# Seven products for eight in the first layer of a four-layer decoder trunk

## The chip, the cores and the metric

The kernel runs on one core of one Trainium2 chip. The metric is device time in microseconds (us) of one execution. The engines are named as the profile names them: PE is TensorE (matmuls, with PEld for the loads of its stationary operand), DVE is VectorE, ACT is ScalarE, POOL is GpSimd, and SP is SyncE, which here issues all the DMAs.

## The reference, cut to what matters

Four residual layers with different token mixers work on x of 1024 tokens by 1024 features. The change touches the first one, the gated convolution mixer:

```python
def conv_mixer(h, w_in, w_conv, w_out):
    proj = h @ w_in                                   # 1024 x 1024 by 1024 x 4096
    b_gate, c_gate, v, z = jnp.split(proj, 4, axis=-1)
    y = b_gate * causal_conv(c_gate * v, w_conv)      # 3 taps along the tokens
    return (y * jax.nn.silu(z)) @ w_out

def reference(x, ...):
    for i in range(DEPTH):
        h = rms_norm(x, norm_w[i])
        ...
        x = x + y.astype(x.dtype)
    return rms_norm(x, final_norm_w)
```

## The kernel before

Features lie on partitions and tokens on the free axis. There are 8 chunks of 128 features (`c`), and the tokens fall into two halves of 512 (`HT`). To keep fp32 precision each operand of a projection is split into a rounded high part and a low rest: ACT casts (`whi`, `hhi`), and POOL (for weights, `split_w`, L137) or DVE (for activations, L288) subtracts (`wlo`, `hlo`). A projection of one 128-column slice of weights on one half (`proj_steps`, L153 to L155) is then 8 chunks times 3 matmuls of 512 columns: high by high, high by low, low by high.

`start` loads x, transposes it on PE, normalises it (DVE L281, ACT L283, DVE L288) and leaves `hhi`, `hlo` for both halves; the first half's are ready first, and PE begins on it while DVE normalises the second.

`layer_conv` goes over 8 feature chunks `f` of the layer's width. For each it projects c, v, b and z on both halves, 8 projections in all. ACT copies c out of PSUM (`cs`, L451), DVE multiplies v by it (`u`, L456), ACT and DVE apply the three taps (L461 to L463), DVE multiplies by b (L468), ACT applies SiLU to z (L476) and DVE writes the gated result into `Y` (L477). The input x waits in DRAM (`xd`, `residual`) for the output projection. During `f == 2` `rope_tables` computes tables for layer 4 on DVE and ACT.

In the last chunk ACT and DVE split the finished `Y` into `hhi`, `hlo` again (`split_y`), and `out_half` projects them with `w_out`; its first three projections take the 7 chunks that are ready before the eighth.

Weights pass through pools of fixed depth: three raw tiles (`wraw`), six pairs `whi`, `wlo` (`WB = 6`), and PSUM has three `pj` tiles, two `sc`, one `ov` and two `tr`. Each engine runs its instructions strictly in the order written down for it. A scheduler writes that order when the program is built; in `start` and in the output projection the order on PE (in `start` that on ACT and DVE too) follows the code.

## Time and profile before

| | before |
|---|---|
| time, median of 3 runs | 2196.29 us (2195.63 to 2200.45) |
| profiled execution: time / span | 2195.09 / 2193.3 us |
| PE busy | 2110.1 us, 96% of the span, 11861 matmuls |
| DVE busy | 1235.0 us, 56% |
| ACT busy | 952.0 us, 43% |
| POOL busy | 784.7 us, 36% |

The span runs from the first to the last instruction; the profiled execution took 1.79 us more than its span. Matmuls overlap in the pipeline, so a matmul's own duration is longer than the distance from one start to the next, and it is that distance which adds up. DVE instructions overlap in the same way by a little: the distance between two starts is the cost of one in a row of them.

### The profile page before, as it was taken

How to read it: one execution, taken by the hardware profiler on the slowest of the kernel's cores; microseconds unless marked ns; L12 is line 12 of the kernel's file. 1: busy time of each engine (PE TensorE's matmuls, PEld its weight loads, DVE VectorE, ACT ScalarE, POOL GpSimd, SP SyncE). 2: the span in 40 equal slices, each digit the busy share in tenths (PEclk: the TensorE clock that was granted, in tenths of full speed). 3: DMA queues.
4: the chain of work that ended last, by engine and by line, in shares of the span. 5: the costliest groups of instructions: out<-in, count | busy, mean ns of one | idle time of the engine just before them, and what ended most of it. 6: DMA issues, size and time to landing. Idle time of an engine off the chain costs nothing.

```text
span 2193.3 us, 33426 instructions
## 1 busy us (share of the span) xinstructions
PE 2110.1 (96%) x11861; PEld 1776.1 (81%) x11861; DVE 1235.0 (56%) x2752; ACT 952.0 (43%) x2407; POOL 784.7 (36%) x685
## 2 busy tenths in 40 slices
PE   8999999999999999999999889999999998988998
PEld 6888888788898989888687677788887787777788
DVE  6141213452635445375454968775566658898874
ACT  6222113432433333354365443434444456666764
POOL 2222222651122121235355653322325544444630
PEclk9999999999999999999999999999999999999999
DMA  6121112551121321135356563333325421111124
GB/s 223 57 72 48 49 48 62 185 140 38 39 48 39 38 54 35 47 99 171 90 150 193 152 178 94 100 102 90 96 74 183 146 66 44 44 49 44 44 80 152
DMA packets 285772, 200.97 MB, mean 92 GB/s; under 512 B 41093, under 2 KB 245286, under 8 KB 285606
## 3 DMA queue, kind: packets, MB, share of 16 engines
q1 hardware_dynamic: 285606, 198.84, 31.9%
q8 instruction: 94, 1.54, 0.3%
q14 instruction: 72, 0.59, 0.1%
HBM read 152.51 MB, written 41.03 MB: 88 GB/s over the span
## 4 chain that ended last, share of the span: by engine, by line
PE 73%; DVE 13%; DMA 5%; ACT 3%; issue 3%; POOL 2%; SPq 1%; ACTq 0%; POOLq 0%; DVEq 0%
PE ps_pj L153 18%; PE ps_pj L154 18%; PE ps_pj L155 18%; PE ps_tr L647 1%; PE ps_pj L555 1%; PE ps_pj L557 1%; PE ps_pj L556 1%; DVE cu L1120 1%; DVE sp L1241 1%; DVE lg L963 1%; PE ps_tr L1135 1%; PE ps_ov L660 1%; PE ps_ov L659 1%; DMA acc<-ra 1%; DVE ra L776 1%
## 5 line engine op out<-in xcount | busy, mean ns | idle before, releaser
L153 PE MATMUL ps_pj<-hhi,whi 128*128 128x512 f32 (+2 forms) x2096 | 849.9, 406 | 1.8 <-ACT hhi L283 0.9
L154 PE MATMUL ps_pj<-hlo,whi 128*128 128x512 f32 (+2 forms) x2096 | 819.8, 391 | 3.6 <-DVE hlo L211 2.9
L155 PE MATMUL ps_pj<-hhi,wlo 128*128 128x512 f32 (+2 forms) x2096 | 819.4, 391 | 0.0
L137 POOL TENSOR_TENSOR wlo<-wraw,whi 128x512 fp32r<-128x512 f32 x308 | 419.5, 1367 | 782.5 <-ACT whi L136 773.7
L155 PEld LDWEIGHTS ps_pj<-hhi,wlo 128*128 128x128 f32 (+1 forms) x2096 | 394.8, 188 | 84.6
L154 PEld LDWEIGHTS ps_pj<-hlo,whi 128*128 128x128 f32 (+1 forms) x2096 | 396.2, 189 | 73.1 <-DVE hlo L211 4.6
L153 PEld LDWEIGHTS ps_pj<-hhi,whi 128*128 128x128 f32 (+1 forms) x2096 | 395.8, 189 | 72.3 <-issue 1.9
L136 ACT CAST whi<-wraw 128x512 fp32r<-128x512 f32 (+1 forms) x316 | 193.5, 617 | 379.5 <-PE ps_pj L154 288.2
L1120 DVE SCALAR_TENSOR_TENSOR cu<-cb,taps,cu 128x512 f32<-128x512 f32 x144 | 134.5, 934 | 12.2 <-ACT cu L1118 10.3
L972 POOL TENSOR_TENSOR lg<-lg,st 128x512 f32<-128x512 f32 (+1 forms) x64 | 64.1, 1002 | 119.8 <-DVE st L971 71.1
L700 ACT ACTIVATE lg<-lg,mx 128x512 f32<-128x512 f32 (+2 forms) x96 | 58.7, 613 | 64.6 <-DVE mx L695 64.3
L966 ACT ACTIVATE lg<-lg,st 128x256 f32<-128x256 f32 (+1 forms) x128 | 62.8, 491 | 49.8 <-DVE st L963 48.4
L652 ACT CAST phi<-ps_tr 128x512 fp32r<-128x512 f32 (+1 forms) x80 | 40.6, 544 | 94.8 <-PE ps_tr L647 94.8
L332 DVE TENSOR_TENSOR y<-ps_pj,xr 128x512 f32<-128x512 f32 x56 | 38.5, 688 | 73.1 <-PE ps_pj L155 61.5
L456 DVE TENSOR_TENSOR u<-ps_pj,cs 128x512 f32<-128x512 f32 x16 | 11.1, 691 | 114.9 <-PE ps_pj L155 112.3
L653 DVE TENSOR_TENSOR plo<-ps_tr,phi 128x512 fp32r<-128x512 f32 (+1 forms) x80 | 49.5, 633 | 42.5 <-ACT phi L652 42.5
L340 DVE TENSOR_TENSOR acc<-acc,hf 128x512 f32<-128x512 f32 x49 | 52.0, 1061 | 37.8 <-ACT hf L339 37.7
L986 PE MATMUL ps_ov<-phi,vv 128*128 128x256 f32 x120 | 32.7, 293 | 29.4 <-DVE o L993 27.8
L1241 DVE TENSOR_TENSOR sp<-sT,sU 128x504 f32<-128x504 f32 (+18 forms) x80 | 56.6, 707 | 6.4 <-DMA sU<-gLT 5.3
L963 DVE CUSTOM_DVE_ANT_0 lg<-ps_sc,band,sk 128x256 f32<-128x256 f32 (+1 forms) x128 | 54.9, 464 | 6.3 <-PE ps_sc L959 4.5
L477 DVE TENSOR_TENSOR y<-t,sz 128x512 f32<-128x512 f32 x16 | 15.9, 994 | 69.1 <-ACT sz L476 69.0
L555 PE MATMUL ps_pj<-whi,hhi 128*128 128x256 f32 x192 | 54.8, 285 | 0.0
(365 smaller groups left out, 3889.0 us busy)
## 6 DMA issues: line engine op xcount, KB each, us to landing
wraw<-in_conv_w_in_dram SPq DMA_DIRECT2D x64, 256.0 KB, 2.8
xd<-y SPq DMA_DIRECT2D x64, 256.0 KB, 3.4
wraw<-in_fox_w_in_dram SPq DMA_DIRECT2D x60, 256.0 KB, 4.2
xr<-xd SPq DMA_DIRECT2D x56, 256.0 KB, 3.0
wraw<-in_gdn_w_in_dram SPq DMA_DIRECT2D x52, 256.0 KB, 3.5
wraw<-in_swa_w_in_dram SPq DMA_DIRECT2D x40, 256.0 KB, 3.0
wraw<-in_conv_w_out_dram SPq DMA_DIRECT2D x32, 256.0 KB, 3.1
wraw<-in_fox_w_out_dram SPq DMA_DIRECT2D x32, 256.0 KB, 2.9
```

What stands on the lines that cost most here:

```text
L136: nc.scalar.copy(hi[:, :, :cols], raw[:, :, :cols])
L137: (eng or nc.gpsimd).tensor_tensor(lo[:, :, :cols], raw[:, :, :cols], hi[:, :, :cols].bitcast(F32), op=ALU.subtract)
L153: nc.tensor.matmul(o, hi, xhi, start=(c == 0), stop=False)
L154: nc.tensor.matmul(o, hi, xlo, start=False, stop=False)
L155: nc.tensor.matmul(o, lo, xhi, start=False, stop=(c == NC_ - 1))
L555: nc.tensor.matmul(ps, xhi, whi, start=(c == 0), stop=False)
L700: nc.scalar.activation(lg[:, :w], lg[:, :w], AF.Exp, bias=m, scale=-1.0, accum_out=su[:, t:t + 1])
L963: nc.vector.tensor_tensor_reduce(lg[:, u, :n], ps[:, u, :n], band[:, 2 * P - n:], 1.0, sk[:, 1, hd:hd + 1], ALU.add, ALU.min, st[:, 0, u:u ...
L966: nc.scalar.activation(lg[:, u, :n], lg[:, u, :n], AF.Exp, bias=st[:, 0, u:u + 1], scale=-1.0, accum_out=st[:, 1, u:u + 1])
L972: nc.gpsimd.tensor_tensor(lg[:, :, :n], lg[:, :, :n], st[:, 3, :].unsqueeze(2).broadcast_to([P, 2, n]), op=ALU.mult)
L1120: eng.scalar_tensor_tensor(u, cb[:, j:j + HT], tap(j), u, op0=ALU.mult, op1=ALU.add)
L1241: nc.vector.tensor_tensor(v, T[:, n0:i, n0:n1].rearrange("p j n -> p n j"), U[:, n0:i, i].unsqueeze(1).broadcast_to([P, n, m]), op=ALU.mult)
```

## The change

The first two feature chunks stay as they were. For the other six, the projections are taken two at a time (c with v, then b with z), and each pair is computed as a product of 2 by 2 blocks: the weight matrix falls into input halves (chunks 0 to 3, chunks 4 to 7) by two slices, and the activations into the same input halves by the two token halves. Strassen's method in Winograd's form does this with seven products of 12 matmuls where eight stood (`quad_steps`); a pair on both halves is called a quad here.

The sums that it needs are made elsewhere. Four mixtures of activations (`mixtures`, 16 pairs of a high and a low tile) are made once, on DVE with ACT's casts, from the normalised fp32 activations: those of the second half are kept (`self.last`), those of the first are computed again from `Y` and the kept row of scales (`self.rb`). They stand in the place of `Y` and of x's tiles. Four mixtures of weights per quad are made by DVE (`split_quad`), and each of the seven operands is split by ACT and POOL as weights were before. The products are summed in PSUM where they can be, and else by ACT copies and DVE additions (`p1`, `p5`, `u2`).

Since `Y` is taken, the gated results of the first two chunks and of all second halves go to DRAM (`yd`) and come back during the last quad; five first halves are kept in tiles of `hhi`, `hlo` that the quads no longer read. All eight chunks of x are written to `xd` at once, before the first chunk. `rope_tables` moves to `f == 3`.

```diff
+    def mixtures(self, p, layer):
+        nc = self.nc
+        self.mix = [[], [], [], []]
+        m0 = []
+        def first_half(c, t):
+            nc.vector.scalar_tensor_tensor(t, self.Y[c][0], self.col("norm_w", layer * NC_ + c), self.rb[0],
+                                           op0=ALU.mult, op1=ALU.mult)
+            return t
+        def keep(m, t, hi, lo):
+            nc.scalar.copy(hi, t)
+            nc.vector.tensor_tensor(lo, t, hi.bitcast(F32), op=ALU.subtract)
+            self.mix[m].append((hi, lo))
...
+        for i in range(4):
+            t = first_half(i, self.tmp("xr" if i % 2 else "hf", 2))
+            nc.vector.tensor_tensor(t, self.last[i], t, op=ALU.subtract)
+            m0.append(t)
+            keep(0, t, *(self.place("y", i, half, F32R) for half in range(NH)))
+            yield
+        for i in range(4):
+            h10 = first_half(i + 4, p.tile([P, HT], F32, name="e", bufs=EB))
+            nc.vector.tensor_tensor(m0[i], self.last[i + 4], m0[i], op=ALU.subtract)
+            keep(1, m0[i], *(self.place("y", i + 4, half, F32R) for half in range(NH)))
+            yield
+            nc.vector.tensor_tensor(h10, h10, m0[i], op=ALU.subtract)
+            keep(3, h10, *wide())
+            yield
+        m2 = []
+        for i in range(4):
+            m2.append(self.tmp("xr" if i % 2 else "hf", 2))
+            nc.vector.tensor_tensor(m2[i], self.last[i + 4], self.last[i], op=ALU.subtract)
+        yield
+        for i in range(4):
+            keep(2, m2[i], *wide())
+            yield
+    def raw_quad(self, p, src, a, b):
...
+        own = lambda: p.tile([P, 4, P], F32, name="wr", bufs=4)
+        shared = lambda: self.wp.tile([P, 4, P], F32, name="wraw", bufs=3)
+        return [load(own(), 0, a), load(shared(), 1, b), load(own(), 0, b), load(shared(), 1, a)]
+    def split_quad(self, p, raws):
+        a0, b1, b0, a1 = raws
+        yield self.split_w(a0, P)
+        s1 = p.tile([P, 4, P], F32, name="ws", bufs=2)
+        nc.vector.tensor_tensor(s1, b0, b1, op=ALU.add)
+        yield self.split_w(s1, P)
+        nc.vector.tensor_tensor(b0, a0, b0, op=ALU.subtract)
+        nc.vector.tensor_tensor(a0, s1, a0, op=ALU.subtract)
+        yield self.split_w(a0, P)
+        yield self.split_w(a1, P)
+        yield self.split_w(b0, P)
+        nc.vector.tensor_tensor(a1, a1, a0, op=ALU.subtract)
+        yield self.split_w(a1, P)
+        yield self.split_w(b1, P)
+    def quad_steps(self, p, ws):
...
+        def product(ps, x, start, stop):
+            whi, wlo = next(ws)
+            for c in range(4):
+                xhi, xlo = x[c]
+                nc.tensor.matmul(ps, whi[:, c, :], xhi, start=start and c == 0, stop=False, skip_group_check=True)
+                nc.tensor.matmul(ps, whi[:, c, :], xlo, start=False, stop=False, skip_group_check=True)
+                nc.tensor.matmul(ps, wlo[:, c, :], xhi, start=False, stop=stop and c == 3, skip_group_check=True)
+        X = self.psum("sc", 2)
+        product(X, h(lo4, 0), True, True)
+        p1 = e()
+        nc.scalar.copy(p1, X)
+        yield None
+        Z = self.psum("pj")
+        product(Z, self.mix[0], True, True)
+        p5 = e()
+        nc.scalar.copy(p5, Z)
+        yield None
+        product(X, self.mix[1], False, True)
+        u2 = e()
+        nc.scalar.copy(u2, X)
+        yield None
+        Y = self.psum("pj")
+        product(Y, h(hi4, 0), True, True)
+        nc.vector.tensor_tensor(p1, Y, p1, op=ALU.add)
+        yield 0, p1
+        product(X, self.mix[2], False, True)
+        nc.vector.tensor_tensor(p5, X, p5, op=ALU.add)
+        yield 3, p5
+        product(Z, h(hi4, 1), False, True)
+        nc.vector.tensor_tensor(u2, Z, u2, op=ALU.add)
+        yield 1, u2
+        product(X, self.mix[3], False, True)
+        yield 2, X
 def layer_conv(k, out):
...
+        for c in (0, 4, 1, 5, 2, 6, 3, 7):
+            k.residual(c)
+        mixing = k.mixtures(p, 0)
+        mix = lambda n: [next(mixing, None) for _ in range(n)]
+        for f in range(2):
...
+                ts.append(t)
+                mix(f)
                 ps = k.proj(w["b"], h)
                 nc.vector.tensor_tensor(t, ps, t, op=ALU.mult)
+                mix(2 * f + h)
+            for h in range(2):
...
+                finish_y(f, h, ts[h], sz)
+                mix(3)
+        mix(20)
+        raws = k.raw_quad(p, w_in, 1024 + 2 * P, 2048 + 2 * P)
+        with k.tc.manual_schedule(engines={mybir.EngineType.PE}):
+            quads = [(f, q) for f in range(2, NC_) for q in range(2)]
...
+                    if not more:
+                        if j == 2:
+                            for g in range(7):
+                                k.Y[g] = [k.place("y", g, h) for h in range(NH)]
+                                nc.sync.dma_start(out=k.Y[g][1], in_=yd[1][g])
+                            for g in range(2):
+                                nc.sync.dma_start(out=k.Y[g][0], in_=yd[0][g])
+                        if j == 3:
+                            for g in (2, 3, 4, 5, 6, 0, 1):
+                                k.split_y(g, 0, y=homes.get(g))
```

Three places show what the new order is.

DVE, where the normalisation of the second half of the tokens begins. `hlo_1_92` and `hlo_1_94` are the low parts of its first two chunks, `y_1_108` and after it its transposed inputs. L281 and L288 of before are L408 and L415 of after; L173, L188 and L179 of after belong to the mixtures. Before:

```order
L194 TENSOR_TENSOR hf<-ident,rs 128x512
L288 TENSOR_TENSOR hlo_0_105<-cs,hhi_0_89 128x512
L281 SCALAR_TENSOR_TENSOR sz<-y_1_108,par,ps_tr 128x512
L281 SCALAR_TENSOR_TENSOR t<-y_1_110,par,ps_tr 128x512
L288 TENSOR_TENSOR hlo_1_92<-sz,hhi_1_76 128x512
L281 SCALAR_TENSOR_TENSOR cs<-y_1_112,par,ps_tr 128x512
L288 TENSOR_TENSOR hlo_1_94<-t,hhi_1_78 128x512
```

After:

```order
L173 SCALAR_TENSOR_TENSOR hf<-y_0_111,par,ps_tr 128x512
L173 SCALAR_TENSOR_TENSOR xr<-y_0_113,par,ps_tr 128x512
L408 SCALAR_TENSOR_TENSOR xb<-y_1_108,par,ps_tr 128x512
L408 SCALAR_TENSOR_TENSOR xb<-y_1_110,par,ps_tr 128x512
L188 TENSOR_TENSOR hf<-xb,hf 128x512
L188 TENSOR_TENSOR xr<-xb,xr 128x512
L415 TENSOR_TENSOR hlo_1_92<-xb,hhi_1_76 128x512
L408 SCALAR_TENSOR_TENSOR xb<-y_1_112,par,ps_tr 128x512
L415 TENSOR_TENSOR hlo_1_94<-xb,hhi_1_78 128x512
L584 TENSOR_TENSOR u<-ps_pj,e 128x512
L179 TENSOR_TENSOR y_1_641<-hf,y_0_640 128x512
L188 TENSOR_TENSOR hf<-xb,hf 128x512
```

The mixtures stand among the low parts for which PE waits: four in this piece ahead of the first, and ten between the first and the last of the eight.

DVE, in the chunk that computes the tables for layer 4 (L911 to L926 of after, L724 to L739 of before). Before, this is the piece that ends with the evacuation of b (L468):

```order
L734 SCALAR_TENSOR_TENSOR rt_nn<-rt_an 128x512
L462 SCALAR_TENSOR_TENSOR t<-u,par,t 128x512
L724 CAST rt_an<-rt_pi 128x512
L463 SCALAR_TENSOR_TENSOR t<-u,par,t 128x512
L736 SCALAR_TENSOR_TENSOR rt_nn<-rt_nn,frq,rt_s_1094 128x512
L725 TENSOR_SCALAR rt_an<-rt_an,frq 128x512
L445 MEMSET u 128x2
L738 TENSOR_TENSOR rt_s_1094<-rt_s_1094 128x512
L468 TENSOR_TENSOR t<-ps_pj,t 128x512
```

After, the piece that ends with L270, the addition that reads X in PSUM before PE may add the seventh product to it:

```order
L226 TENSOR_TENSOR wr<-wr 128x512
L921 SCALAR_TENSOR_TENSOR hf<-xr 128x512
L911 CAST xr<-acc 128x512
L912 TENSOR_SCALAR xr<-xr,frq 128x512
L923 SCALAR_TENSOR_TENSOR hf<-hf,frq,xr 128x512
L267 TENSOR_TENSOR e<-ps_pj,e 128x512
L914 TENSOR_SCALAR hf<-xr 128x512
L925 TENSOR_TENSOR xr<-xr 128x512
L661 TENSOR_TENSOR t<-t,e 128x512
L915 TENSOR_SCALAR hf<-hf 128x512
L926 TENSOR_SCALAR xr<-xr 128x512
L270 TENSOR_TENSOR e<-ps_sc,e 128x512
```

The tables' instructions now stand ahead of an instruction that PE waits for in the same quad.

ACT, in the last chunk, where the finished results are split for the output projection (`split_y`, L177 of before, L296 of after). Before:

```order
L461 ACTIVATE t<-u,par 128x512
L177 CAST hhi_0_75<-y_0_107 128x512
L177 CAST hhi_0_77<-y_0_109 128x512
L177 CAST hhi_0_79<-y_0_111 128x512
L177 CAST hhi_0_81<-y_0_113 128x512
L177 CAST hhi_0_83<-y_0_115 128x512
L177 CAST hhi_0_85<-y_0_117 128x512
L177 CAST hhi_0_87<-y_0_119 128x512
L476 ACTIVATE sz<-ps_pj 128x512
```

After, where L259 is the copy of the second product, L263 that of X after the third, and `y_1_2804`, `y_0_2803`, `y_1_2807` and `y_1_2810` are tiles that come back from DRAM:

```order
L254 COPY e<-ps_sc 128x512
L296 CAST hhi_0_81<-hhi_1_1707 128x512
L296 CAST hhi_1_2920<-y_1_2804 128x512
L141 CAST whi<-wraw 128x512
L259 COPY e<-ps_pj 128x512
L296 CAST hhi_0_75<-y_0_2803 128x512
L296 CAST hhi_1_2922<-y_1_2807 128x512
L296 CAST hhi_1_2924<-y_1_2810 128x512
L141 CAST whi<-wraw 128x512
L263 COPY e<-ps_sc 128x512
```

Copies of PSUM for which PE waits now stand behind casts that wait for DMAs.

## Rows read from the trace of the kernel before

**Rows 1.** The page: span, busy time by engine (share, count), clock by slice.

```profile
span 2193.3 us, 33426 instructions
PE 2110.1 (96%) x11861; PEld 1776.1 (81%) x11861; DVE 1235.0 (56%) x2752; ACT 952.0 (43%) x2407; POOL 784.7 (36%) x685
```

**Rows 2.** Stretches: length, busy time (count) by engine, granted clock, DMA share, GB/s.

```profile
10.00:12.00 2.00, 0.65 (x4) 0.27 (x2) 1.47 (x6) 1.03 (x2) 1.02 (x1) 1.00 0.86 242
14.00:16.00 2.00, 1.08 (x5) 0.68 (x4) 1.12 (x3) 2.00 (x5) 0.77 (x1) 0.50 0.97 320
18.00:20.00 2.00, 2.00 (x6) 1.52 (x6) 2.00 (x4) 2.00 (x6) 0.00 (x0) 0.50 1.05 396
40.00:50.00 10.00, 9.17 (x41) 7.43 (x40) 10.00 (x13) 6.05 (x12) 3.90 (x2) 1.00 0.37 133
50.00:100.00 50.00, 50.00 (x222) 41.40 (x221) 10.88 (x16) 12.85 (x20) 14.36 (x11) 1.00 0.20 59
```

**Rows 3.** Timeline of PE: start, duration, line, operands; first and last of 117 matmuls.

```profile
354.66 0.39 PE L153 MATMUL ps_pj<-hhi,whi 128*128 128x512 f32 x1
...
380.95 0.39 PE L155 MATMUL ps_pj<-hhi,wlo 128*128 128x512 f32 x1
```

**Rows 4.** Groups by line, 50 to 350 us: operation, count, busy, mean ns, idle before.

```profile
L137 POOL TENSOR_TENSOR wlo<-wraw,whi 128x512 fp32r<-128x512 f32 x57 | 74.5, 1308 | 227.0 <-ACT whi L136 223.8 <-PE ps_pj L155 3.2
L477 DVE TENSOR_TENSOR y<-t,sz 128x512 f32<-128x512 f32 x14 | 14.5, 1038 | 69.0 <-ACT sz L476 69.0
L468 DVE TENSOR_TENSOR t<-ps_pj,t 128x512 f32<-128x512 f32 x14 | 9.6, 689 | 35.8 <-PE ps_pj L155 35.8
L451 ACT COPY cs<-ps_pj 128x512 f32<-128x512 f32 x15 | 8.7, 582 | 31.5 <-PE ps_pj L155 31.5
```

**Rows 5.** Timeline of DVE and POOL, 33 to 58 us.

```profile
33.08 0.75 DVE L281 SCALAR_TENSOR_TENSOR sz<-y,par,ps_tr 128x512 f32<-128x512 f32 x1 [3.07 <-ACT y L254]
39.20 0.68 DVE L288 TENSOR_TENSOR hlo<-cs,hhi 128x512 fp32r<-128x512 f32 x1
39.80 0.74 DVE L281 SCALAR_TENSOR_TENSOR t<-y,par,ps_tr 128x512 f32<-128x512 f32 x1
40.46 0.68 DVE L288 TENSOR_TENSOR hlo<-sz,hhi 128x512 fp32r<-128x512 f32 x1
44.91 2.43 POOL L137 TENSOR_TENSOR wlo<-wraw,whi 128x512 fp32r<-128x512 f32 x1 [15.45 <-ACT whi L136]
46.10 1.78 DVE L463 SCALAR_TENSOR_TENSOR t<-u,par,t 128x512 f32<-128x512 f32 x1
47.81 1.77 DVE L288 TENSOR_TENSOR hlo<-t,hhi 128x512 fp32r<-128x512 f32 x1
57.70 0.69 DVE L468 TENSOR_TENSOR t<-ps_pj,t 128x512 f32<-128x512 f32 x1 [1.42 <-PE ps_pj L155]
```

**Rows 6.** The chain that ended last, in order of time, 17 to 27 us.

```profile
17.31 6.14 DMA wraw<-in_conv_w_in_dram
...
23.47 0.62 ACT whi L136
...
24.65 1.37 DVE hlo L288
...
26.06 0.51 PE ps_pj L154
```

**Rows 7.** Timeline of PE and ACT: a wait that ends, and casts in a row.

```profile
41.05 0.50 PE L153 MATMUL ps_pj<-hhi,whi 128*128 128x512 f32 x1 [0.83 <-ACT cs L451]
38.40 0.62 ACT L283 CAST hhi<-cs 128x512 fp32r<-128x512 f32 x1
38.92 0.59 ACT L254 COPY y<-ps_sc 128x512 f32<-128x512 f32 x1
```

**Rows 8.** DMA: transfers from DRAM to tile (page), and those of tile xd, 0 to 60 us.

```profile
xr<-xd SPq DMA_DIRECT2D x56, 256.0 KB, 3.0
DMA to landing us min/median/max: 2.0/5.1/7.4
```

More of the change, by code (lines that the diff above doesn't have):

```diff
@@ L76, in __init__, with place @@
         nc.vector.memset(self.mhalf, -0.5)
+    def place(self, nm, c, h, dt=F32):
+        return self.act.tile([P, HT], dt, name=f"{nm}{c}_{h}")
     def params(self):
@@ new lines, in quad_steps @@
+    def quad_steps(self, p, ws):
+        nc = self.nc
+        h = lambda cs, half: [(self.hhi[c][half], self.hlo[c][half]) for c in cs]
+        lo4, hi4 = range(4), range(4, 8)
+        e = lambda: p.tile([P, HT], F32, name="e", bufs=EB)
+        def product(ps, x, start, stop):
[31 more added lines that the diff above has]
+        yield 2, X
@@ L171, in gate2_steps, with split_y @@
         nc.vector.scalar_tensor_tensor(y, y, 1.0, ps, op0=ALU.add, op1=ALU.mult)
[L174 removed]
+    def split_y(self, c, half, eng=None, y=None):
         nc = self.nc
[L176 removed]
+        y = self.Y[c][half] if y is None else y
         nc.scalar.copy(self.hhi[c][half], y)
@@ L279, in start @@
                     if c < NC_:
-                        hf = st.tile([P, HT], F32, name=next(scratch), bufs=2)
+                        if half:
+                            if c % 2 == 0:
+                                wide = st.tile([P, D], F32, name="xb", bufs=8)
+                            hf = self.last[c] = wide[:, c % 2 * HT:(c % 2 + 1) * HT]
+                        else:
+                            nm = next(scratch)
+                            hf = st.tile([P, HT], F32, name=nm, bufs=bufs[nm])
                         nc.vector.scalar_tensor_tensor(
@@ L440, in layer_conv @@
             w = {}
-            for n in names:
-                c0 = off[n] * 1024 + f * P
+            for n, off in (("c", 1), ("v", 2), ("b", 0), ("z", 3)):
+                c0 = off * 1024 + f * P
                 w[n] = k.pre.pop(0) if k.pre else k.load_w(w_in[:, c0:c0 + P])
-            u = p.tile([P, S + 2], F32, name="u")
-            nc.vector.memset(u[:, 0:2], 0.0)
-            taps = [k.col("conv_w_conv", j * NC_ + f) for j in range(3)]
-            def one_c(h):
+            u, ts = new_u(), []
```

151 lines of the change are left out of this document (95 added, 56 removed).

## The prediction

> **What bounds the kernel now.** I read the page first: PE is busy 96% of the span [rows 1]. Busy time alone can hide a slow engine, so I looked at the stretches next. From 50 us on PE is busy for the whole 50 us at the granted clock 1.00 (2.4 GHz), while DVE works 10.9, ACT 12.9 and POOL 14.4 us of them [rows 2]. What is worth something there is a matmul less, and nothing else. The price of a matmul is the distance between starts: from 354.66 to 380.95 us lie 116 of them [rows 3], so (380.95 - 354.66) / 116 = 0.2266 us. Before 50 us it is different: from 40 to 50 us DVE is busy 10.00 of 10.00 us, PE 9.17 [rows 2]. There the second half of the tokens is normalised, and DVE has no room.
>
> **Matmuls removed.** Before, six chunks take 6 x 8 projections of 24 matmuls = 1152; after, 12 quads of 7 products of 12 = 1008. Gain: 144 x 0.2266 = **32.6 us**, all on PE's path. That the order has 144 rows less on PE (9866 to 9722) shows that nothing is added to them. Here the Trainium skill differs: "TensorE: Matmul & The Clock Gate", section "Back-to-back issue gap", gives about 131 ns as the sustained distance of matmuls of 512 columns, by which the gain would be an estimated 18.9 us. The row has 0.2266 with nothing idle, so the row decides.
>
> **The quads themselves: nothing.** A quad takes PE 84 x 0.2266 = 19.0 us, a product 2.72. POOL has 14 splits per chunk, 14 x 1.31 = 18.3 us of 38.1 [rows 4], and even with every one at 2.43 [rows 5] 34.0. DVE has 24 instructions, about 17 with two operands in SBUF: at the slowest row, 1.78 [rows 5], and 0.69 for the other seven [rows 4], 35.1 us, still under 38.1. So neither engine's sum bounds a chunk. What can stop PE is the reuse of a PSUM tile: X may take its third, fifth and seventh product only after ACT or DVE has read it, and one product on another tile, 2.72 us, stands between. On ACT one cast stands ahead of the copy: 0.52 [rows 7] + 0.58 [rows 4] = 1.1. On DVE one instruction can stand ahead: 1.78 + 0.69 = 2.5. Both fit into 2.72. I take 0. If a second slow instruction stood ahead, each quad would lose 1.78 + 1.78 + 0.69 - 2.72 = 1.5 us, the upper end, 18 us for twelve.
>
> **The start, DMA.** PE's chain at 17 us is a weight load that lands after 6.14 us, its cast, the low part, and a matmul at 26.06 [rows 6]. In the new order two of the first quad's weight loads stand ahead of it on SP, in place of one load of positions: 256 KB more on DMA engines that move 396 GB/s at a share of 1.05 [rows 2]. That is **0.7 us**, between 0 and 2.7 (all four early quad loads, 1.05 MB). The residual writes are the same bytes as before. The 9 tiles that go to DRAM and come back meet a DMA share of 0.20 [rows 2] and cost nothing but in the last quad, below.
>
> **The start, DVE.** In a row of DVE instructions a subtraction costs 0.60 us (39.20 to 39.80) and a scaled multiply 0.66 [rows 5]. Four mixture multiplies fall into the 3.07 us in which DVE was idle before 33.08 and cost nothing. Twelve subtractions stand among the eight low parts, 12 x 0.60 = 7.2 us. Laid out from the first L408 at 33 us, the low parts of chunks 2 to 7 come at 41.0, 44.1, 46.6, 49.1, 51.6 and 52.8; add 0.7 for the DMA, and 1.04 (1.78 - 0.74) for a POOL split near 48. PE comes to the second half at about 40 (41.05 less its wait of 0.83 [rows 7]); eight transposes moved behind that point make it 39.3. With the matmuls ahead of each, PE asks for chunk 4 at 46.8 and has it at 47.3, and asks for chunk 5 at 48.7 and has it at 50.3. Then 19 matmuls of b, 4.3 us, cover the rest. Loss **2.1 us**; ends 0 (the slack holds all) and 7.2 (none does). ACT's casts for these mixtures fit beside the 6.05 us that it works from 40 to 50 [rows 2]. The other 24 mixture instructions lie in the some 60 us until the first quad. DVE has 48 instructions there; at 1.04 each [rows 4] that is 50 us, so they cost nothing. One of them adds a wait: L224, the first sum of weights, waits for two loads, some 3.0 us [rows 8], and the readings of v and b in PSUM are queued behind it; PE asks for such a tile again two projections, 10.9 us, after it is full, so the wait is covered. Without that cover it would cost 3.0.
>
> **The tables for layer 4.** They now lie in the chunk f == 3. When its first quad has completed X, DVE must reach L270 of the second within six products, 16.3 us. Counted in the new order, 28 instructions stand between, 16.0 us at the undisturbed distances: just in time, before any disturbance. Six splits of POOL fall into that time; if half of them cost 1.04, L270 is late by **2.8 us**. Ends 0 and 5.9 (all six). Before, the tables hid in PE's time, and no evacuation had so short a date.
>
> **The last quad.** From its start at T, PE ends its products at 2.72, 5.44, 8.16 and 10.88. The tiles into which the results come back are free from T + 3.4 on, but the reloads stand on SP behind a `w_out` load that waits for POOL's last split, at 2.72 + 0.6 + 0.6 + 1.3, about 5.4. The first lands 3.0 us later [rows 8], about 9. ACT runs eight instructions from that cast to L263, X's copy: 9 + 8 x 0.55 = 13.4, and PE may add the fifth product. PE has 3 matmuls of the output projection in between, 10.88 + 0.68 = 11.6. Loss **2.0 us**; with landing at 2.0 or 7.4 [rows 8] 0.8 or 6.2. After that 43 matmuls of the early projections, 9.7 us, cover the last chunk's split.
>
> **Sum.** -32.6 + 0.7 + 2.1 + 2.8 + 2.0 = -25.0 us. On the profiled execution's own time, 2195.09 (span 2193.3 and 1.8 around it), that is 2170.1; the median is 1.2 above that execution, so I predict **2171 us**.
>
> **Rivals.** (a) *Every wait is absorbed*: the orders hold in practice, and only matmuls count: 2196.3 - 32.6 = 2164. For it: the slack at the tables and the start is short by only a few us. Against it: DVE had none from 40 to 50 us.
>
> (b) *A POOL split holds DVE for its whole overlap*. L477, with both operands in SBUF, averages 1.04 us, L468, with one in PSUM, 0.69 [rows 4]; L463 took 1.78 while a split took 2.43 [rows 5]. If each split that meets such an instruction costs 1.04, one more in the start (+1.0) and all six at the tables (+3.1) give 2175, and with a queue behind them up to 2180. By the Trainium skill, "SBUF — State Buffer", section "Who interferes with whom", a VectorE instruction with two SBUF inputs and a GpSimd instruction that reads SBUF exclude each other for a whole instruction; the rows agree in kind, L468 staying at 0.69.
>
> (c) *DVE late in every quad*: 12 x 1.5 = 18 us: 2189. Against it: the order puts L270 with at most one instruction between it and L267.
>
> (d) *Slower than before: the clock.* From 10 to 12 us PE was busy 0.65 of 2.00 us, and then ran at 0.50, 1.2 GHz, from 14 to 20 [rows 2]. If each quad had a wait of that 1.35 us and then lost 3 us (6 us at half the clock), 12 x 4.35 = 52 us: 2171 + 52 = 2223. It decides from 12 x 2.1 us on, since only 25 are to be lost. Against it: I find no wait of that length in an ordinary quad.
>
> That the change does not do what it says is excluded by the 144 rows.
>
> **How the numbers follow.** Forecast, 2166 to 2174: 0.55. (a) 2162 to 2166: 0.12. (b) 2174 to 2181: 0.15. (c) 2181 to 2191: 0.08. Between 2192 and 2201: 0.03. (d) and beyond: 0.07. The range 2163 to 2183 holds the forecast, most of (a) and (b), a piece of (c): 0.8. A difference of 0.2%, 4.4 us, is about what a measurement tells from none. Faster 0.90, same 0.03, slower 0.07.
>
> **What would show it.** Matmul starts stay 0.2266 apart in the quads at clock 1.00; PE's idle time in the layer should be in three places: before a low part of the second half (near 47 to 51 us), before the seventh product of the quad that follows c and v of f == 3, and before the fifth product of the last quad, on L263. Right in sum but wrong in place would be idle time spread over all quads (c). The prediction fails if DVE's low parts come over 5 us late, or if the granted clock falls in the quads.

## The result and the profile after

The changed kernel takes **2171.69 us** (median of four runs, 2170.40 to 2174.69), the kernel before 2197.70 beside it (2195.63 to 2200.45): 0.9883 of it, 95% interval 0.9866 to 0.9900, or 26.0 us less. Forecast were 2171. The profiled execution took 2172.09, with a span of 2170.4. Its page, to be read beside [rows 1]:

```profile
span 2170.4 us, 33535 instructions
PE 2086.8 (96%) x11717; PEld 1753.5 (81%) x11717; DVE 1347.4 (62%) x2876; ACT 993.1 (46%) x2483; POOL 838.4 (39%) x721
```

PE has 144 matmuls less, as the order said, and 23.3 us less busy time; DVE, off the path, has 112 us more. The stretches of the changed kernel, in the columns of [rows 2]:

```profile
40.00:50.00 10.00, 7.61 (x38) 5.91 (x37) 10.00 (x14) 5.09 (x9) 2.96 (x2) 1.00 0.32 111
50.00:100.00 50.00, 49.93 (x220) 41.01 (x219) 30.59 (x43) 18.45 (x31) 14.07 (x10) 1.00 0.19 57
100.00:180.00 80.00, 80.00 (x352) 65.71 (x351) 46.96 (x56) 28.13 (x48) 36.75 (x27) 1.00 0.22 66
184.00:188.00 4.00, 3.73 (x11) 3.00 (x12) 3.88 (x8) 1.45 (x3) 1.49 (x1) 0.69 0.13 52
188.00:192.00 4.00, 3.96 (x16) 2.85 (x15) 4.00 (x7) 0.98 (x2) 1.29 (x1) 0.89 0.06 25
192.00:340.00 148.00, 148.00 (x648) 121.20 (x647) 87.75 (x101) 58.61 (x102) 72.08 (x54) 1.00 0.26 78
```

The quads begin at 113.6 us. From 100 to 180 and from 192 to 340 us PE is busy to the last tenth, so an ordinary quad waits for nothing. Time is lost from 40 to 50 us (7.61 of 10) and around 184 us, where the granted clock also leaves 1.00. What PE waits for up to 410 us (line waited for, sum, times, longest, in us):

```profile
...
PE ps_pj L159 <- DVE hlo L415: 3.8, 3, 2.4
PE ps_ov L524 <- DVE acc L468: 2.4, 1, 2.4
PE ps_sc L247 <- ACT e L263: 1.9, 1, 1.9
```

New among these, and over 1 us, are 2.4 us in one piece for a low part of the start (L415) and X's copy on ACT (L263); the wait before the first output projection sum (L524) was there before, too, with 3.6 us. The start first. Timelines of DVE and POOL in the changed kernel, 45 to 49 us, beside [rows 5], and the PE row that waited:

```profile
46.10 1.22 DVE L179 TENSOR_TENSOR y<-xr,y 128x512 fp32r<-128x512 f32 x1
47.24 1.75 DVE L194 TENSOR_TENSOR xr<-xb,xr 128x512 f32<-128x512 f32 x1
48.91 0.68 DVE L415 TENSOR_TENSOR hlo<-xb,hhi 128x512 fp32r<-128x512 f32 x1
```

```profile
45.48 2.96 POOL L142 TENSOR_TENSOR wlo<-wraw,whi 128x512 fp32r<-128x512 f32 x2 [15.66 <-PE ps_pj L159]
```

```profile
49.64 0.50 PE L159 MATMUL ps_pj<-hlo,whi 128*128 128x512 f32 x1 [2.39 <-DVE hlo L415]
```

Two mixture rows, L179 and L194, stand directly ahead of the low part that PE wants, and both are held, to 1.22 and 1.75 us instead of 0.68, while POOL makes two low parts of weights. The second place, the second quad of f == 3, in the timelines of PE, ACT, DVE and POOL:

```profile
184.27 0.50 PE L247 MATMUL ps_sc<-xb,whi 128*128 128x512 f32 x1 [1.91 <-ACT e L263]
...
191.66 0.50 PE L247 MATMUL ps_sc<-xb,whi 128*128 128x512 f32 x1
```

```profile
179.51 0.62 ACT L141 CAST whi<-ws 128x512 fp32r<-128x512 f32 x1 [1.62 <-PE ps_sc L248]
183.12 0.63 ACT L920 ACTIVATE xr<-xr 128x512 f32<-128x512 f32 x1 [2.99 <-DVE xr L917]
183.65 0.57 ACT L263 COPY e<-ps_sc 128x512 f32<-128x512 f32 x1
```

```profile
174.98 1.78 DVE L587 SCALAR_TENSOR_TENSOR t<-u,par,t 128x512 f32<-128x512 f32 x1
...
180.70 1.78 DVE L224 TENSOR_TENSOR ws<-wr,wraw 128x512 f32<-128x512 f32 x1
182.41 0.68 DVE L917 SCALAR_TENSOR_TENSOR xr<-hf,xr 128x512 f32<-128x512 f32 x1
...
190.93 0.68 DVE L270 TENSOR_TENSOR e<-ps_sc,e 128x512 f32<-128x512 f32 x1
```

```profile
174.76 1.45 POOL L142 TENSOR_TENSOR wlo<-wraw,whi 128x512 fp32r<-128x512 f32 x1 [1.50 <-ACT whi L141]
...
180.21 1.72 POOL L142 TENSOR_TENSOR wlo<-ws,whi 128x512 fp32r<-128x512 f32 x1 [1.30 <-ACT whi L141]
```

ACT takes its rows in order. X was complete at 179.5, but ahead of its copy L263 stands the sine L920, and that waits for DVE's third L917, which ends at 183.1. So PE gets the fifth product at 184.27 instead of 182.2. DVE's own L270, which frees X for the seventh product, ends at 191.6; without any wait PE would have asked at 182.2 + 2 x 2.8 = 187.8 us. Both are late, and the trace alone doesn't say which of them is the loss.

**The account.** Times between fixed points of PE's timeline show where the 24.8 us lie by which the first output projection sum comes earlier (L396 at 423.19 before, L524 at 398.36 after). "100th" is the start of the hundredth projection matmul (47.30 us before, 45.94 after; the 200th at 69.97 and 71.67), and so on; the columns on the right are kernels of the next section.

| stretch of PE, us | before | changed | mixtures later | tables spread | both edits |
|---|---|---|---|---|---|
| 1st to 100th projection matmul | 31.57 | 30.65 | 30.61 | 32.72 | 34.36 |
| 100th to 200th | 22.67 | 25.73 | 22.67 | 25.72 | 22.67 |
| 200th to 385th (after: the first quad's start) | 41.93 | 41.93 | 41.93 | 41.93 | 41.93 |
| first quad to the end of the last one's fourth product | | 226.56 | 226.54 | 222.52 | 222.52 |
| from there to the first L524 | | 58.20 | 57.77 | 60.29 | 58.27 |

From the 385th matmul to the output projection the kernel before took 311.29 us, the changed one 284.76: 26.53 less, where the 144 matmuls alone would have given 32.63. In front of it 3.06 us were lost between the 100th and the 200th. The first row is not a matter of the order alone: in the two columns on the right PE also ran at granted clock 0.50 from 28 to 30 us, in the other three at 1.00. Behind the layer nothing was changed, and there two profiles of the same order differ by up to 8 us (1765 to 1773 us from the first L524 to the end over all kernels here); so reasons are read from stretches, and only medians of whole runs are compared.

### The profile page after: what moved, and what is told of

It is laid out like the page before. It is cut to its first block, busy times and chain, and to the rows that moved or that the text cites. A ratio compares the mean times of both kernels' runs of the same rounds, so it can differ in the third digit from the quotient of the medians.

```text
span 2170.4 us, 33535 instructions
## 1 busy us (share of the span) xinstructions
PE 2086.8 (96%) x11717; PEld 1753.5 (81%) x11717; DVE 1347.4 (62%) x2876; ACT 993.1 (46%) x2483; POOL 838.4 (39%) x721
## 4 chain that ended last, share of the span: by engine, by line
PE 71%; DVE 14%; DMA 5%; issue 4%; ACT 3%; POOL 2%; SPq 1%; ACTq 0%; POOLq 0%; DVEq 0%
PE ps_pj L158 14%; PE ps_pj L159 14%; PE ps_pj L160 14%; PE ps_sc L247 2%; PE ps_sc L249 2%; PE ps_sc L248 2%; DVE sp L1428 1%; PE ps_tr L834 1%; DVE cu L1307 1%; PE ps_pj L247 1%; PE ps_pj L248 1%; PE ps_pj L249 1%; PE ps_pj L742 1%; PE ps_pj L744 1%; PE ps_pj L743 1%
## 5 line engine op out<-in xcount | busy, mean ns | idle before, releaser
L158 PE MATMUL ps_pj<-hhi,whi 128*128 128x512 f32 (+1 forms) x1712 | 699.7, 410 | 1.6 <-DVE y L460 0.8
L159 PE MATMUL ps_pj<-hlo,whi 128*128 128x512 f32 (+1 forms) x1712 | 670.9, 392 | 7.2 <-DVE hlo L415 3.8
L160 PE MATMUL ps_pj<-hhi,wlo 128*128 128x512 f32 (+1 forms) x1712 | 670.7, 392 | 0.4 <-DVE wlo L142 0.4
L142 POOL TENSOR_TENSOR wlo<-wraw,whi 128x512 fp32r<-128x512 f32 x296 | 406.4, 1379 | 635.6 <-ACT whi L141 594.5
L160 PEld LDWEIGHTS ps_pj<-hhi,wlo 128*128 128x128 f32 x1712 | 322.6, 188 | 69.9 <-DVE wlo L142 0.8
L159 PEld LDWEIGHTS ps_pj<-hlo,whi 128*128 128x128 f32 x1712 | 323.8, 189 | 62.1 <-DVE hlo L415 5.8
L158 PEld LDWEIGHTS ps_pj<-hhi,whi 128*128 128x128 f32 x1712 | 323.5, 189 | 57.7 <-issue 2.6
L141 ACT CAST whi<-wraw 128x512 fp32r<-128x512 f32 x304 | 186.0, 617 | 323.5 <-PE ps_pj L159 177.8
L468 DVE TENSOR_TENSOR acc<-acc,hf 128x512 f32<-128x512 f32 x49 | 49.4, 1008 | 41.8 <-ACT hf L467 41.8
L142 POOL TENSOR_TENSOR wlo<-wr,whi 128x512 fp32r<-128x512 f32 x36 | 48.0, 1332 | 59.4 <-ACT whi L141 55.2
L290 DVE SCALAR_TENSOR_TENSOR y<-y,ps_pj 128x512 f32<-128x512 f32 x48 | 32.7, 680 | 38.1 <-ACT y L289 38.0
```

Of the source, the lines that this page charges most:

```text
L141: nc.scalar.copy(hi[:, :, :cols], raw[:, :, :cols])
L142: (eng or nc.gpsimd).tensor_tensor(lo[:, :, :cols], raw[:, :, :cols], hi[:, :, :cols].bitcast(F32), op=ALU.subtract)
L158: nc.tensor.matmul(o, hi, xhi, start=(c == 0), stop=False)
L159: nc.tensor.matmul(o, hi, xlo, start=False, stop=False)
L160: nc.tensor.matmul(o, lo, xhi, start=False, stop=(c == NC_ - 1))
```

## Experiments on the tables for layer 4

**ACT's order alone.** One swap: L263 ahead of L920, everything else in the order of the changed kernel.

```diff
-                                    if f == 3 and g == 0:
-                                        with k.tc.issue_after(ins.ins):
-                                            rope_tables(k)
+                                    if f == 3 and g == 0:
+                                        first_u = ins
...
+                    if (f, q, j) == (3, 1, 2): tables_behind(k, first_u, k.u2_copy)
```

> The changed kernel with one swap on ACT: in the second quad of f == 3 the copy of X (L263) stands ahead of the first sine of the tables (L920) instead of behind it; every other engine's order is the same. Theory V (VectorE is late): in the trace of the changed kernel DVE ends L270 at 191.6 us, and has no idle time between 172 and 191 us; PE would ask for it at 187.8 us. Then the wait of 1.9 us at the fifth product goes, but PE waits some 3 to 4 us at the seventh product for L270, and the end of the layer moves by less than 1 us. Rival Q (the queue on ACT is the whole cause): the wait at the fifth product and the half clock behind it go, nothing comes in their place, and the layer ends 4.0 us earlier (the first output projection sum, L524, at 394.3 instead of 398.4).

Measured: 2175.86 us (2171.43 to 2180.34). The wait at the fifth product is gone and stands at the seventh, by PE's and DVE's timelines of this kernel:

```profile
192.81 0.79 PE L247 MATMUL ps_sc<-xb,whi 128*128 128x512 f32 x1 [3.72 <-DVE e L270]
```

```profile
192.08 0.68 DVE L270 TENSOR_TENSOR e<-ps_sc,e 128x512 f32<-128x512 f32 x1
```

From the first quad to the end of the last one's fourth product it takes 227.84 us, 1.3 more than in the changed kernel (under 1 was expected), because the longer wait is followed by half clock and nothing behind it would have made PE wait anyway. Theory V holds and Q falls: DVE's L270 is the loss, and the sine in front of L263 only moved the wait two products ahead.

**Less in DVE's stretch.** Tied to ACT's copy alone, DVE's first half of the tables moves into the plain chunks.

```diff
-                                        with k.tc.issue_after(ins.ins):
-                                            rope_tables(k)
...
+                    if (f, q, j) == (3, 1, 2): tables_behind(k, k.u2_copy)
```

> The changed kernel, but the tables for layer 4 are only tied to ACT's copy L263 of the second quad of f == 3, so that the first half of their VectorE steps (9 rows) falls into the time of the two plain chunks, and about as many fewer stand between the gated product and L270. Theory V (VectorE is late in that stretch): L270 comes 7 to 9 us earlier, PE waits nowhere between 168 and 200 us, the granted clock stays 1.00 there, and the layer ends 4.0 us earlier. Rival Q (only ACT's order counts) gives the same 4.0 us, so the two are told apart by copy_first; a rival by which the weights' low parts from POOL are late would keep the wait. In the plain chunks DVE has room: nothing is lost there.

Measured: 2173.66 us (2169.54 to 2174.52); first quad to last 224.80, 1.8 less than in the changed kernel, not 4.0. A wait remains:

```profile
192.81 0.50 PE L247 MATMUL ps_sc<-xb,whi 128*128 128x512 f32 x1 [2.00 <-DVE e L270]
```

The direction is that of V, the size was wrong: the rows of the second half still stand between the gated product and L270, and three rows there were held to 1.5 to 1.8 us while POOL worked. DVE also stood idle for 2.2 us there until the weight load for L224 had landed (at 182.09 us), so that not all of the room that was made could be used. The wait near 50 us was followed by half clock in this profile (100th to 200th matmul 27.34), 1.6 us more than in the changed kernel, which took back most of what the quads gave.

**Both halves out of the way.**

```diff
-                                        with k.tc.issue_after(ins.ins):
-                                            rope_tables(k)
...
+                    if q and f in (3, 5) and j == 5: half_table(k, k.z_read)
```

> The changed kernel, with the tables for layer 4 in two pieces: the first half is tied behind L273 of the second quad of f == 3, the second half behind L273 of the second quad of f == 5, where VectorE has 12 of its ordinary rows and more than one quad's time until the next L270. Theory V (VectorE has too much to do between the gated product of f == 3 and L270): PE waits nowhere from 170 to 340 us, at no half clock, and the layer ends some 4 us earlier than in the changed kernel (the wait of 2.1 us, 1.6 + 0.4 at half clock, less the 0.2 us of an ordinary quad). Rival (any place in a quad is too short): a wait of 1 to 3 us stands in each of two quads instead.

Measured: 2169.12 us (2165.93 to 2173.78). The stretches of this kernel, in the columns of [rows 2]:

```profile
150.00:200.00 50.00, 50.00 (x220) 40.95 (x219) 32.07 (x39) 17.91 (x31) 24.48 (x18) 1.00 0.25 75
250.00:300.00 50.00, 50.00 (x220) 40.96 (x220) 38.20 (x46) 20.41 (x35) 25.21 (x19) 1.00 0.30 89
```

PE is full in both places that now hold a half, at clock 1.00; first quad to last takes 222.52, so the tables had cost **4.04 us**. The medians lie 2.6 apart and their ranges overlap, so the whole runs alone would not show it. In the layer's last part this profile lost 2 us more than the changed kernel's; that part varies from profile to profile.

**POOL's low parts on DVE.** The seven low parts of weights of the second quad of f == 3 go to VectorE, which is thereby given more to do.

```diff
-                    nxt = k.split_quad(p, raws)
+                    nxt = k.split_quad(p, raws, nc.vector if n + 1 == 3 else None)
```

> The changed kernel, but the seven low parts of weights of the second quad of f == 3 are made on VectorE instead of POOL (the order on ACT then has L263 ahead of L920 too). Theory P (POOL's subtraction holds VectorE): in the trace of the changed kernel six DVE rows between 172 and 191 us took 0.4 to 1.1 us more than their usual time while a POOL row ran, 5.7 us in sum; without POOL rows they take 0.42 to 0.75, and although 7 x 0.60 = 4.2 us of work is added on DVE, L270 comes some 1.5 us earlier than in copy_first. Rival W (VectorE has only too much to do): L270 comes 2.5 to 4.2 us later than in copy_first, and PE waits the longer for it.

Measured: 2168.72 us (2167.99 to 2172.66). From the second L584 to L270 DVE takes 17.2 us (172.01 to 189.22), in the kernel with one swap 19.4 (172.69 to 192.08): 2.2 less, although two low parts are added and three short rows left out, by their distances (2 x 0.60 and 3 x 0.33) 0.2 us more in sum. DVE rows in which the difference lies, of this kernel and then of the one with one swap:

```profile
174.96 0.74 DVE L587 SCALAR_TENSOR_TENSOR t<-u,par,t 128x512 f32<-128x512 f32 x1
...
180.19 0.68 DVE L224 TENSOR_TENSOR ws<-wr,wraw 128x512 f32<-128x512 f32 x1
```

```profile
176.16 1.78 DVE L587 SCALAR_TENSOR_TENSOR t<-u,par,t 128x512 f32<-128x512 f32 x1
...
181.89 1.78 DVE L224 TENSOR_TENSOR ws<-wr,wraw 128x512 f32<-128x512 f32 x1
```

Theory P holds, W falls. Not every held row went: the next quad's low parts, still on POOL, came into the stretch and held four rows for 3.8 us in sum, where it had been six for 5.8. So PE still waited 1.54 us for L270 here, and the quads still lose 2.7 of the 4.04 us against those with the tables spread (first quad to last 225.26). The Trainium skill, "SBUF — State Buffer", section "Who interferes with whom", calls the pair of ports that VectorE and GpSimd share an exclusive lock, over which a VectorE instruction with two inputs in SBUF contends with a GpSimd instruction that reads SBUF. The rows of L587 and L224 above agree: 1.78 us beside POOL's rows, 0.74 and 0.68 without them.

## Experiments on the start

**Mixtures later.**

```diff
-                nc.vector.tensor_tensor(t, ps, t, op=ALU.mult)
-                mix(2 * f + h)
+                b_read = nc.vector.tensor_tensor(t, ps, t, op=ALU.mult)
+                mix_after(k, b_read, mix, f, h)
```

> The changed kernel, but no mixture is begun before VectorE has read the second b projection of f == 0 (near 62 us), so that none stands among the low parts of the second half. Theory M (the mixtures make these late): the wait of 2.4 us near 49.6 us goes, the start ends 2 to 2.5 us earlier (the first quad would begin at 111.2 instead of 113.6 us), and the later mixtures still end before the quads need them, at 113 to 125 us. Rival D (the weight loads in front on SP cause it): the wait stays. Rival L (the mixtures then come late): the wait near 49.6 goes but PE waits in the second, third or fifth product of the first quad.

Measured: 2168.18 us (2163.82 to 2171.71). PE is busy through the place of the wait (stretch of this kernel):

```profile
44.00:50.00 6.00, 6.00 (x28) 4.97 (x27) 3.04 (x4) 2.35 (x5) 2.68 (x2) 1.00 0.39 128
```

The 100th to the 200th matmul takes 22.67 us, as in the kernel before: the mixtures in the start had cost **3.06 us**, and later they cost nothing, since the first quad waits for none. M holds, with one limit: the order on PE follows from the edit and differs in the start, too. This run also separates wait and clock in the quad of the tables, in PE's timeline:

```profile
182.20 0.50 PE L247 MATMUL ps_sc<-xb,whi 128*128 128x512 f32 x1 [1.91 <-ACT e L263]
...
189.58 0.50 PE L247 MATMUL ps_sc<-xb,whi 128*128 128x512 f32 x1 [1.55 <-DVE e L270]
```

The same 1.91 us at the fifth product was not followed by half clock here, so PE came to the seventh earlier and waited 1.55 for L270. The quads take 226.54 us, against 226.56 with half clock: in the changed kernel the low clock fell into a time that L270 would have taken anyway.

**Weight loads behind the residual's writes.**

```diff
-        raws = k.raw_quad(p, w_in, 1024 + 2 * P, 2048 + 2 * P)
+        raws = quad_behind(k, p, w_in)
...
+def quad_behind(k, p, w_in):
+    with k.tc.issue_after(k.last_write.ins):
+        return k.raw_quad(p, w_in, 1024 + 2 * P, 2048 + 2 * P)
```

> The changed kernel, but SP issues the four weight loads of the first quad behind the last write of the residual, so that none stands ahead of the loads with which PE starts. Theory D (these 256 KB delay PE's first weights, the 0.7 us of the prediction): the waits of 0.6 us at 23.5 and 1.1 us at 25.6 us (for a weight's cast and a low part) shrink by 0.7 us together and the first quad begins 0.7 us earlier, at 112.9. Rival: in these stretches PE waits for ACT and VectorE, not for a load; nothing moves by more than the 0.5 us by which the start of the trace differs from run to run. The order of the first matmuls is also somewhat changed, since the order follows from it.

Measured: 2172.05 us (2170.91 to 2174.09). Inconclusive on the loads: the 1st to the 100th matmul took 31.57 us, and seven profiles in which this part stands in the changed kernel's order took 30.65 to 33.12 (31.6 on average, one profile of before 31.57). The spread is larger than the 0.7 in question. The edit also changed the order of the second half: the wait for a low part is only 0.81 us and, with one of 0.22 for DVE's L615, now lies ahead of the 100th matmul, and the 100th to 200th took 23.07.

## Experiments on the quads

**Late release, a small dose.** Two more reads of X on DVE before the seventh product.

```diff
-        nc.vector.tensor_tensor(p5, X, p5, op=ALU.add)
-        yield 3, p5
+        d = self.tmp('acc'); [nc.vector.tensor_tensor(d, X, p5, op=ALU.add) for _ in range(2)]
+        nc.vector.tensor_tensor(p5, X, p5, op=ALU.add); yield 3, p5
```

> The changed kernel, and in every quad VectorE reads the fifth product's tile twice more (into a scratch tile) before L270, so that X is released 1.2 us later. Theory S (slack): in an ordinary quad of the changed kernel L270 ends at 228.48 and the seventh product begins at 230.26, with its tile wanted at 230.0, so 1.5 us are free and twelve quads lose nothing, but a VectorE row held to 1.78 us ahead of it costs some 1 us in a few; sum 0 to 4 us, most of it in the quad of the tables. Rival C (quads have no slack on VectorE): 12 x 1.2 = 14 us more.

Measured: 2177.63 us (2175.62 to 2179.04), 5.9 more, where 0 to 4 were expected. What PE waits for on these lines from 100 to 340 us (L271 is the L270 of the changed kernel, one line further down):

```profile
PE ps_sc L247 <- DVE e L271: 5.6, 1, 5.6
PE ps_sc L247 <- ACT e L263: 1.9, 1, 1.9
```

One wait, in the quad of the tables (a second of 1.2 us in the last quad), none in the others: S holds, C falls. The quad of the tables alone took 5.8 us longer than in the changed kernel, 29.06 for 23.26. An ordinary quad has at least the 1.2 us of the two reads to spare on VectorE.

**Late release, a large dose.** The same with five reads.

```diff
-        ... for _ in range(2)]
+        ... for _ in range(5)]
```

> The changed kernel, and in every quad VectorE reads the fifth product's tile five times more before X is released; by the order on VectorE the last two of the six reads stand behind L273, so that PE waits at the seventh product until three rows after the sixth product's end, about 2.0 us in each of 12 quads, 24 us. Two theories on what such a wait does: theory K (the clock stays): granted clock 1.00 in the quads and 2172 + 24 = 2196 us; theory H (each wait is followed by half clock, as rival (d) of the prediction says, with 3 us lost each time): the clock falls to 0.5 in each quad for a while and the time is 2172 + 12 x 5 = 2232 us. In the trace of the changed kernel the wait of 1.9 us at 184.27 us was followed by half clock until 188.5; in the one where the mixtures were moved the same wait was followed by none, so something between is likely.

Measured: **2229.07 us** (2225.74 to 2234.28), 1.0154 of the kernel before, interval 1.0137 to 1.0171: slower than before. Waits, and stretches of an ordinary quad of this kernel:

```profile
PE ps_sc L247 <- DVE e L271: 36.5, 11, 7.8
```

```profile
132.00:136.00 4.00, 1.32 (x6) 0.76 (x5) 3.71 (x6) 0.62 (x1) 1.27 (x1) 1.00 0.35 97
136.00:138.00 2.00, 2.00 (x7) 1.51 (x6) 0.00 (x0) 0.00 (x0) 0.00 (x0) 0.50 0.23 69
138.00:140.00 2.00, 2.00 (x7) 1.60 (x6) 0.25 (x1) 0.53 (x1) 0.00 (x0) 0.65 0.00 0
```

An ordinary quad waits 2.7 or 3.2 us (2.0 were expected; the last reads stand behind L273 and, in a quad of b and z, behind one row more) and then runs at 0.50, some 3.5 us long, which costs some 1.8. The ten ordinary quads that wait follow each other in 23.6 to 24.5 us instead of 19.24, 4.7 each, 47 in sum. The quad of the tables, which waits 2.0 and 7.8 us, takes 33.48 for 23.26, 10.2 more, and the last one loses nothing: 47 + 10 = 57, the difference of the medians. H holds in kind, K falls; the half clock cost 1.8 us each time and not 3.

**Where an operand lies.** The quad takes 19.22 us, not 84 x 0.2266 = 19.03.

```diff
-            keep(0, t, *(self.place("y", i, half, F32R) for half in range(NH)))
+            keep(0, t, *wide())
...
-            keep(3, h10, *wide())
+            keep(3, h10, *(self.place("y", i, half, F32R) for half in range(NH)))
```

> The changed kernel with the places of two sets of mixtures exchanged: those of the second product in the wide xb tiles, those of the seventh in the y tiles. In the changed kernel every fifth and seventh product (xb) takes 2.80 to 2.82 us for its 12 matmuls and every other one 2.72, 0.2 us in a quad, 2.4 us in twelve. Theory T (the place of the operand): the second product takes 2.80 and the seventh 2.72. Rival A (adding to X, the products' place in the quad): the second stays at 2.72 and the seventh at 2.80.

The starts of the second and third product and of the seventh and the next quad's first, in PE's timeline of this kernel:

```profile
117.88 0.39 PE L247 MATMUL ps_pj<-xb,whi 128*128 128x512 f32 x1
120.68 0.39 PE L247 MATMUL ps_sc<-y,whi 128*128 128x512 f32 x1
...
131.68 0.39 PE L247 MATMUL ps_sc<-y,whi 128*128 128x512 f32 x1
134.40 0.39 PE L247 MATMUL ps_sc<-hhi,whi 128*128 128x512 f32 x1
```

The second now takes 2.80 us and the seventh 2.72: T holds. Matmuls whose moving operand is in an xb tile start 0.2333 us apart, 0.2266 with an operand in y, hhi or hlo. Why is open: the xb tiles are also twice as wide and hold the high and the low part side by side, and no run tells the place from that. The one run of 2175.40 us says nothing more, since the y tiles are now wanted longer and the last quad's reloads come late (a wait of 2.8 us for ACT's L296 at 353 us).

## Versions that beat both

**Both edits** (mixtures later, tables in two halves).

> The changed kernel with the two edits that the traces spoke for: no mixture before VectorE's second b reading of f == 0, and the tables in two halves behind L273 of the second quads of f == 3 and f == 5. If the two losses are independent, their measured sizes add: 3.1 us from the 100th to the 200th projection matmul (25.7 to 22.7) and 4.0 us from the first quad to the last (226.6 to 222.5): 2172 - 7 = 2165 us. Rival: with the one wait gone another takes its place, and the gain is 3 to 4 us, 2168.

Measured: **2165.19 us** (2164.37 to 2166.23), 0.9867 of the kernel before, interval 0.9848 to 0.9887. The stretches show 22.67 and 222.52 us: the two gains add, 3.06 + 4.04 = 7.1 us; by the medians 6.5.

**A thirteenth quad**, b and z of f == 1, with both edits.

```diff
...
-            quads = [(f, q) for f in range(2, NC_) for q in range(2)]
+            quads = [(1, 1)] + [(f, q) for f in range(2, NC_) for q in range(2)]
```

> As the kernel with both edits, and b and z of f == 1 are a thirteenth quad, in front of the others: 12 matmuls less, 12 x 0.2266 = 2.7 us. Theory: the mixtures are ready in time (the last of them ends near 100 us in the changed kernel, and this quad asks for its first at about 94, its third set at 102 and its fourth at 107 us), so that 2165 - 2.7 = 2162 us. Rival: mixtures begun only near 62 us are some 9 us later than in the changed kernel, PE waits 3 to 10 us for the mixtures of the fifth or seventh product, and nothing or less than nothing is left of the 2.7.

Measured: 2166.90 us (2164.99 to 2173.12), no gain. PE's timeline of this kernel:

```profile
102.05 0.79 PE L247 MATMUL ps_sc<-y,whi 128*128 128x512 f32 x1 [3.21 <-ACT e L254]
```

The rival was right, at another row: not a mixture, but X's first copy L254, which is queued on ACT; the wait comes at the third product and half clock follows.

**The same with the first quad's loads behind the writes.**

> As the kernel with thirteen quads, but SP issues this first quad's weight loads behind the residual's last write. In the changed kernel that edit gave 2.7 us from the 100th to the 200th matmul by another order of the second half, which the later mixtures already give; so here it should bring only what the loads cost in front, 0 to 1 us: 2161 to 2162. Rival: the loads come too late for the quad's first splits and cost 1 us or more.

Measured: 2163.03 us (2162.19 to 2166.40), 0.9861, interval 0.9841 to 0.9881; 3.9 less than with thirteen quads alone, where up to 1 was expected. The wait for L254 is 2.24 us, and no half clock follows:

```profile
98.52 0.50 PE L247 MATMUL ps_sc<-y,whi 128*128 128x512 f32 x1 [2.24 <-ACT e L254]
```

It is the fastest median here, but its range meets that of the version with both edits, so the gain over that one is not shown.

## Why the prediction was right, point by point

**Matmuls, -32.6: right.** The quads' matmuls start 0.2266 us apart (but for the xb tiles), and from the 385th matmul to the output projection PE saves 26.53 us, which with the tables' 4.0 and the xb tiles' 2.4, below, makes 33.0. The estimate by the Trainium skill's 131 ns ("TensorE: Matmul & The Clock Gate", section "Back-to-back issue gap"), 18.9 us, is borne out by no run.

**Quads, 0: the waits right, a term missing.** No ordinary quad waits, and even 1.2 us of delay is covered. But 24 matmuls of each quad cost 0.0067 us more, 0.2 us with the first row behind: **2.4 us** in twelve that I had not thought of. The step that failed is "84 x 0.2266": I took the distance from matmuls with other operand tiles.

**Start, DMA, +0.7: not settled.** The spread of the profiles, 2.5 us, is as wide as the bounds 0 to 2.7, and the one of the changed kernel was even 0.9 faster here than the one of before. The prediction also has this 0.7 twice: it moves the low parts in the next term, and PE's dates there are not moved with it.

**Start, DVE, +2.1: right in kind and place, too small.** The wait was forecast before low parts near 47 to 51 us and stands at 49.64; the loss is 3.06. I had let it fall on two chunks with 0.5 and 1.6. It came in one piece, behind two rows that POOL held there (1.6 us by their durations) where I had counted one (1.04); no run took POOL's rows out of the start. That part is rival (b), and where it was tested, at the tables, it is true: POOL's row holds DVE's row. The other 24 mixture rows in the plain chunks cost nothing, 41.93 us before and after; there L224's wait for its loads stayed covered too.

**Tables, +2.8: the cause right, the size too small, the first wait elsewhere.** L270 was late, but by 3.8 us (191.6 for 187.8): of the six low parts of POOL that I had counted, with half of them in the sum, every one held a row, 5.8 us together. The step that failed is the 16.0 us for the 28 rows: they took 20.1 us from the second L584 (171.50) to the end of L270, so 14.3 without what POOL held. Too long a queue and too few held rows made 2.8 together; 14.3 with half the low parts would have given 1.1, so the nearness of this term is luck in part. And PE stopped first at the fifth product, on ACT: I had counted DVE's queue, and not the sine in ACT's queue ahead of L263, whose input is made by DVE. The swap shows that this set the place: without it the wait stands at the seventh product and the sum is no smaller (1.3 us more). The sum is **4.04 us**.

**Last quad, +2.0: wrong, 0.** SP's and ACT's rows, and the PE row:

```profile
331.24 0.37 SPq L131 DMA_DIRECT2D wraw<-in_conv_w_out_dram  x1
332.65 0.34 SPq L671 DMA_DIRECT2D y<-yd  x1
```

```profile
339.53 0.58 ACT L263 COPY e<-ps_sc 128x512 f32<-128x512 f32 x1
```

```profile
340.84 0.39 PE L247 MATMUL ps_sc<-xb,whi 128*128 128x512 f32 x1
```

The quad begins at T = 329.26. I had the `w_out` load wait until T + 5.4 and the reloads behind it; it went at T + 2.0 and the first reload at T + 3.4, when its tile was free. So L263 ended at T + 10.9, not T + 13.4, 0.7 us before PE asked. The failed step is the date of the load's tile on POOL: the low part that released it ended at 331.21, T + 2.0. The prediction's own terms also add up to less than it took from them: 2.72 + 0.6 + 0.6 + 1.3 is 5.2, and with 3.0 and 8 x 0.55 that is 12.6, a loss of 1.0 us. The margin is small: with the tables spread, one profile waited 0.46 us for L263 here.

**Sum.** 3.1 for the start, 4.0 for the tables and 2.4 for xb make 9.5 against the 7.6 forecast. From the 1st to the 100th matmul this profile gained 0.9, ahead of that 0.4, and at the layer's end 0.3, none of which I had forecast: -32.6 + 9.5 - 1.6 = -24.7, where -24.8 was measured up to the output projection. The forecast of -25.0 was met with two terms too small, one too large and one missing, and with 1.6 us that differ from profile to profile; so that it came this near is luck in part. Of the three waits that were to take back part of the 32.6, two came and one didn't.

**Rivals.** (a) falls: the losses are there. (b) is right as a mechanism, and its sum, 2175 to 2180, was too high because the tables cost 4.0 and not 5.9 us and the last quad nothing. (c) falls by the small dose. (d), slower than before, did not happen. When the quads were made to wait, the kernel was slower than before, at 4.7 us per quad where 4.35 were priced; but that nearness is luck, since the waits were 2.7 to 3.2 us and not 1.35, and the half clock cost 1.8 and not 3. The waits of 1.55 us (mixtures later) and 1.54 us (low parts on DVE) for L270 were not followed by half clock. What kept (d) away is the spare time of an ordinary quad, at least 1.2 us.

## What to carry to other kernels

When an engine gets new rows, ask for every in-order queue which row stands ahead of the one that frees PE's tile, and which engine makes that row's input; then move the new rows behind the last date of a quad rather than ahead of it. Taking one wait away shows at once whether another stands behind it, and only the latest one is the loss. Where a tensor product is cut to fewer but tighter steps, most of what is left of the gain hangs on a microsecond or two of slack in each step.
